# A bidirectional pooling and recurrence block on one core: stores issued by GpSimd, gate and pool products one step later, sums of the last rows made ahead

## The chip, the core and the metric

The kernel runs on one core of a Trainium2 chip. The core has five engines that work side by side, each on its own list of instructions and in the order of that list: TensorE (PE, with PEld for its weight loads), VectorE (DVE), ScalarE (ACT), GpSimd (POOL) and SyncE (SP), which here only issues transfers. An engine that issues a transfer does so in the order of its list as well: when the transfer has to wait for its data, all that stands behind it in that list waits too. The metric is the device time of one execution in microseconds, as the median of a few runs.

## What is computed

One encoder layer over 2048 positions of width 2048, all in float32. Cut to what matters:

```python
h = rms_norm(x, norm_g) * (1 + scale) + shift          # shift, scale, gate = silu(c) @ w_ada + b_ada
z = h @ w_in + b_in                                    # 2048 x 2048 @ 2048 x 4096
u_pool, u_lru, g_pool, g_lru = split(z)                # 1024 columns each
y_pool = pool_mixer(u_pool, w_pool, ...)               # 4 groups of 256: window mean, minus u, @ w_pool
y_lru  = bidir_rg_lru(centred_dwconv(u_lru, ...), ...) # 4 heads of 256: gates = uh @ w_gate, forward + backward scan
y = concat(rms_norm(y_pool) * silu(g_pool), rms_norm(y_lru) * silu(g_lru)) @ w_out + b_out
out = rms_norm(x + gate * y, final_norm_g)             # 2048 x 2048 @ 2048 x 2048
```

## The kernel before

Every product of float32 numbers is made of three: each operand is split into a rounded upper part and the rest (ScalarE copies with rounding, VectorE subtracts, L179 and L180 for the moving operand `m`, L327 and L328 for the stationary operand `s`), and `mm3` (L331) multiplies upper by upper, upper by rest and rest by upper.

**Steps.** One loop runs over `t`, 352 steps of 24 matmuls of 128x512: four output tiles, two slices of the contraction, three products. Steps 0 to 127 make the first half of the input product (four groups of 256 columns of u with their gates), steps 128 to 239 the second half, steps 240 to 351 the output product. The two latter parts save one product in eight by Strassen's method as Winograd wrote it: seven products of half-size blocks (`PRODUCTS`, L134), 56 steps for one pair of column blocks, each product `k` for two halves `q` of the moving side in four slices `p`. `sg` counts the four such sets: 0 and 1 for the input, 2 and 3 for the output. The sums that they need are made by VectorE: of the moving operands in `combine` (L272), of the stationary ones in `unit_split` (L304), of the results in `in_evac` (L478) and `out_evac` (L775). Sums that are used again go to HBM and are loaded back.

**Side work.** The function `at(t, fn, ...)` puts work behind the matmuls of step `t`. A unit of the recurrence (`lru_unit`, L542: one head, direction and block of 512 positions) convolves and splits its input into the only buffer `uch` at step b, multiplies it by the gate weights on TensorE at b+1 and b+2 (`gates`, into the two PSUM buffers `px`), and scans on VectorE at b+4. A unit of the pooling (`pool_unit`, L649) makes window sums at b, multiplies at b+1 (`mix`) and ends at b+2 (`fin`). `rn` (L953) makes the row factors of the group norms, `gate_rows` (L763) spreads the gate over the partitions by four small matmuls. Within its list an engine's order is set at build time by a scheduler with a model of its own, so side work can stand some matmuls before or after where the loop put it.

**Buffers and queues.** `raw` is a ring of eight 512 KB tiles: every load of the loop goes into one, and the results that VectorE makes in place are stored from one, which comes free when the store has landed. SP issues all loads and nearly all stores. Stores of VectorE's results are gathered in a list `late` and issued by SP at the next step, behind that step's loads (L1016 and L1017); ScalarE issues the stores of its own results. Accumulators lie in six PSUM buffers `pm` and two `px`; a product takes four of them, and a buffer is taken again when `in_evac` or `out_evac` has read it. Only in set 3 products 1 and 6 go on adding in the buffers of products 0 and 5 (`CHAINED`, L135), and the second halves `q` use both `px`.

**The end.** After the last product's last step, `out_evac` (L775) adds each of four output tiles to its row block, `part_fin` (L823) multiplies the last quarter of the row by the gate and adds x (which already holds the bias), ScalarE squares and sums it, and `out_row` (L834) scales by the norm and stores.

Of the kernel before, what the change touches and what calls it, by code (L numbers as in the profile page):

```python
# [10 lines left out]
AF = mybir.ActivationFunctionType  # L11
# [34 lines left out]
def layer(ctx: ExitStack, tc: tile.TileContext, xc, xn, c, wada, win, wgate, wpool, wout, vecs, consts, bout, fng, out):  # L46
# [225 lines left out]
    def combine(proj, k, p, q):  # L272
        a, b = wraw.pop(("t", k, q, 0)), wraw.pop(("t", k, q, 1))
        vtt(out=a, in0=a, in1=b, op=ALU.subtract)  # L274
        late.append((moving(proj, f"T{k + 1}", p, q), a))


    rn_t = {}
    late = []

# [18 lines left out]
    def normed(r, tb, k, p):  # L299
        for j in range(2):  # L300
            vtt(out=r[:, j], in0=r[:, j], in1=rn_t[tb, "PL"[k]], op=ALU.mult)  # L301
        late.append((yscr[PAIRS[p + 4 * k]][tb], r))

    def unit_split(u):  # L304
        sg, name, p = unit_args(u)
        rs = yraw.pop(u)
        r = rs[0]
        tb = 2 * (sg - 2)
        if name in ("A11", "A12"):
            if sg > 1:  # L310
                normed(r, tb, int(name[2]) - 1, p)
        elif name == "S2":
            r = rs[1]
            if sg > 1:
# [5 lines left out]
            late.append((sscr[0][p], rs[2]))  # L320
            late.append((sscr[1][p], r))
# [137 lines left out]
    def evac_fix(g, tb):  # L459
        r = R_t.pop(tb)[:, :TB]  # L460
        gr = g_t.pop((g, tb))
        for n in range(4):
            dst = u_t[g][n][:, usl(tb)] if n < 2 else gr[:, n - 2]
            vtt(out=dst, in0=dst, in1=r, op=ALU.mult)
        late.append((gscr[g][tb], gr))

# [11 lines left out]
    def in_evac(sg, k, q, banks):  # L478
# [6 lines left out]
        for n, ps in enumerate(banks):  # L485
            g, i = 4 + 2 * sg + n // 2, n % 2
            bu, bg_ = V("b_in", 4 * g + i), V("b_in", 4 * g + 2 + i)
            lo, hi = u_t[g][i][:, usl(q)], u_t[g][i][:, usl(q + 2)]
            if k == 0:
                act(out=hi, in_=ps, func=AF.Copy)  # L490
            elif k == 1:
                stt(out=lo, in0=ps, scalar=bu, in1=hi, op0=ALU.add, op1=ALU.add)
            elif k == 2:
                vtt(out=hi, in0=ps, in1=hi, op=ALU.add)
            elif k == 3:
                vtt(out=U3[q][:, n], in0=ps, in1=hi, op=ALU.add)
            elif k == 4:
                if i == 0:
                    g_t[g, q] = raw("gr")
                stt(out=g_t[g, q][:, i], in0=U3[q][:, n], scalar=bg_, in1=ps, op0=ALU.add, op1=ALU.subtract)  # L500
                if i == 1:
                    late.append((gscr[g][q], g_t.pop((g, q))))
            elif k == 5:
                stt(out=U3[q][:, n], in0=ps, scalar=bg_, in1=U3[q][:, n], op0=ALU.add, op1=ALU.add)
                vtt(out=hi, in0=ps, in1=hi, op=ALU.add)
                if i == 1:
                    late.append((gscr[g][q + 2], U3[q][:, n - 1:n + 1]))
            else:
                stt(out=hi, in0=ps, scalar=bu, in1=hi, op0=ALU.add, op1=ALU.add)
# [32 lines left out]
    def lru_unit(g, h, d, tb, b, last):  # L542
# [48 lines left out]
        def scan():  # L591
# [21 lines left out]
            if d == 0:  # L613
                late.append((hscr[h][tb], st["h"]))

# [6 lines left out]
        def merge():  # L622
# [4 lines left out]
            for i in range(2):  # L627
# [3 lines left out]
                vtt(out=v, in0=v, in1=hf[:, i], op=ALU.add)  # L631
            late.append((yscr[g][tb], gr))
            if last:
# [4 lines left out]
        at(b, split)  # L638
        at(b + 1, gates, 0)
        at(b + 2, sig, 0)  # L640
        at(b + 2, gates, 1)
        at(b + 3, sig, 1)
        at(b + 3, expo)
        at(b + 4, scan)
        if d == 1:
            at(b + 3, reload)
            at(b + 5, merge)

    def pool_unit(g, q, tb, b, last):  # L649
# [51 lines left out]
        def fin():  # L701
# [7 lines left out]
            for m in range(2):  # L709
# [4 lines left out]
                vtt(out=v, in0=v, in1=y, op=ALU.add)  # L714
            late.append((yscr[g][tb], gr))

        at(b, sums)
        at(b + 1, mix)
        at(b + 2, fin)

# [54 lines left out]
    def out_evac(sg, k, q, banks, tiles):  # L775

        lo, hi = (slice((q + 2 * h) * TB, (q + 2 * h + 1) * TB) for h in range(2))
        for n in tiles:
# [16 lines left out]
            else:  # L795
                vtt(out=b[:, hi], in0=ps, in1=b[:, hi], op=ALU.add)
                if not sg:
                    vtt(out=a[:, hi], in0=ps, in1=a[:, hi], op=ALU.add)

# [23 lines left out]
    def part_fin(sg, n, h, lo, hi, slot):  # L823
# [7 lines left out]
        if hi == 1024:  # L831
            del x_t[sg, n, h]

    def out_row(sg, n, slots, parts):  # L834
        i = row_of(sg, n)
# [8 lines left out]
        for q in range(parts):  # L844
# [4 lines left out]
            else:  # L849
                late.append((out[i * 128:(i + 1) * 128, ds], o))  # L850

# [27 lines left out]
    def gate_fin():  # L879
# [6 lines left out]
    L_AT = {0: [47 + 5 * i for i in range(8)], 2: [87 + 5 * i for i in range(8)],  # L886
            3: [128 + 11 * i // 2 for i in range(8)], 4: [172, 182] + [188 + 5 * i for i in range(6)]}
    P_AT = {1: (75, 80, 85, 90), 5: (164, 180, 184, 186), 6: (221, 236, 242, 248), 7: (224, 239, 245, 251)}
    units = []
# [60 lines left out]

    rn_at = [(228, 0, "P"), (229, 0, "L"), (230, 1, "L"), (231, 2, "L"), (232, 3, "L"), (242, 1, "P"), (248, 2, "P"), (254, 3, "P")]

# [7 lines left out]
    for i in range(4):  # L960
        at(257 + i, gate_rows, i)

# [21 lines left out]
    for t in range(NT):  # L984
# [47 lines left out]
        if key not in banks:  # L1032
            if t == 0:
                banks[key] = [px(), px(), pm(), pm()]
            else:
                banks[key] = [px(), px(), pm(), pm()] if t >= T1 and sg == 3 and q else [pm() for _ in range(4)]
        bk = banks[key]
# [4 lines left out]
        if last:  # L1042
            if t < T1 or sg < 3 or k not in CHAINED.values():
                del banks[key]
# [86 lines left out]
```

## Time and profile before

| | |
|---|---|
| runs, us | 2218.67, 2220.7, 2225.88 (median 2220.7) |
| profiled execution, us | 2217.44 |
| its span, first to last instruction, us | 2215.4 |
| granted TensorE clock, mean | 0.994 |
| TensorE matmul, busy | 2166.2 us, 98% |
| VectorE, busy | 1802.0 us, 81% |
| ScalarE, busy | 1255.3 us, 57% |
| GpSimd, busy | 6.2 us |
| HBM traffic over the span | 276 GB/s |

The profile is one execution. Busy time of TensorE says little by itself, since matmuls are pipelined: one that begins late is seen in the waits and in the distance from start to start. A view of waits lists idle time of an engine by the instruction that ended it; for SP it is the time that its list stood still. "SPq" is an instruction with which SP issues a transfer. A line such as L1017 can stand for many transfers, told apart by the names out<-in.

### The profile page before, as it was taken

The page shows a single profiled execution, that of the slowest core. Times are in us where ns is not written, and L with a number is a line of the kernel's source. Part 1 is how long each engine was busy: PE and PEld are TensorE (multiplying, and loading weights), DVE is VectorE, ACT ScalarE, POOL GpSimd, SP SyncE. Part 2 cuts the span into 40 slices and gives each one's busy share as a digit, 9 for nine tenths or more (in the row PEclk, how much of TensorE's full clock was granted, in tenths as well). Part 3 has the DMA queues.
Part 4 walks back from the last instruction along what each step waited for, and adds up shares of the span by engine and source line. Part 5 has one row for each costly group of instructions (what it writes and reads, how often), then busy time and mean ns, then how long its engine had stood idle before and what let it go on. Part 6 is the DMA issues. An engine that isn't in the chain of part 4 may idle for free. (4 is left out here: it accounts for less than half of the span.)

```text
span 2215.4 us, 25700 instructions
## 1 busy us (share of the span) xinstructions
PE 2166.2 (98%) x9448; PEld 1775.4 (80%) x9448; DVE 1802.0 (81%) x2178; ACT 1255.3 (57%) x1552; POOL 6.2 (0%) x40
## 2 busy tenths in 40 slices
PE   7999999999999999999999999999999999999997
PEld 6888888878788887888888787877877888888886
DVE  7999766578986786867898877979887779967688
ACT  4555578677766676566756666644543333433232
POOL 0000000000000000000000000000000000000000
PEclk9999999999999999999999999999999999999999
DMA  9879945668988897885887787798678756887664
GB/s 389 337 280 334 329 157 200 244 209 294 326 301 311 320 327 278 310 312 200 306 314 257 272 310 275 246 344 297 236 243 308 246 194 235 323 313 289 205 231 171
DMA packets 161342, 613.22 MB, mean 277 GB/s; under 512 B 17856, under 2 KB 19136, under 8 KB 153280
## 3 DMA queue, kind: packets, MB, share of 16 engines
q1 hardware_dynamic: 154880, 588.51, 74.2%
q10 hardware_dynamic: 6336, 23.07, 2.7%
q8 instruction: 74, 1.21, 0.2%
q14 instruction: 52, 0.43, 0.1%
HBM read 467.85 MB, written 143.65 MB: 276 GB/s over the span
## 5 line engine op out<-in xcount | busy, mean ns | idle before, releaser
L334 PE MATMUL pm<-m,s 128*128 128x512 f32 x8004 | 1857.8, 391 | 7.9 <-DVE sum L788 7.9
L334 PEld LDWEIGHTS pm<-m,s 128*128 128x128 f32 x8004 | 1506.3, 188 | 330.7 <-DVE sum L788 8.7
L179 ACT ACTIVATE m<-xr 128x1024 fp32r<-128x1024 f32 x350 | 369.3, 1055 | 499.0 <-PE pm L334 323.1
L180 DVE TENSOR_TENSOR m<-xr,m 128x1024 fp32r<-128x1024 f32 x350 | 426.9, 1221 | 131.9 <-ACT m L179 125.2
L334 PE MATMUL px<-uch,gw 128*128 128x512 f32 x768 | 191.4, 394 | 9.4 <-ACT uch L563 5.2
L334 PEld LDWEIGHTS px<-uch,gw 128*128 128x128 f32 x768 | 143.6, 189 | 45.6 <-DVE uch L564 8.4
L327 ACT ACTIVATE s<-yr 128x1024 fp32r<-128x1024 f32 x104 | 109.5, 1054 | 92.3 <-DMA yr<-in_win_dram 27.1
L328 DVE TENSOR_TENSOR s<-yr,s 128x1024 fp32r<-128x1024 f32 x104 | 126.9, 1221 | 22.3 <-ACT s L327 22.3
L334 PE MATMUL px<-m,s 128*128 128x512 f32 x420 | 105.0, 394 | 13.0 <-ACT m L383 12.4
L402 DVE CUSTOM_DVE_ANT_0 ada<-ada,cact 128x2048 f32<-128x2048 f32 x47 | 107.4, 2288 | 10.4 <-DMA ada<-in_wada_dram 10.4
L274 DVE TENSOR_TENSOR tr<-tr 128x1024 f32<-128x1024 f32 x64 | 78.3, 1224 | 45.3 <-DMA tr<-xs 16.9
L334 PEld LDWEIGHTS px<-m,s 128*128 128x128 f32 x420 | 79.1, 190 | 30.6 <-ACT m L383 12.4
L579 DVE TENSOR_TENSOR ig<-ig,u 128x512 f32<-128x512 f32 x64 | 44.2, 691 | 36.8 <-ACT ig L577 36.8
L598 DVE SCALAR_TENSOR_TENSOR th<-rg,th 128x512 f32<-128x512 f32 x64 | 42.7, 686 | 36.6 <-ACT th L593 36.6
L195 ACT ACTIVATE xr<-xr,shv 128x512 f32<-128x512 f32 x64 | 44.0, 717 | 24.6 <-DVE xr L194 23.5
L334 PE MATMUL px<-uch,pw 128*128 128x512 f32 x192 | 50.0, 398 | 5.1 <-ACT uch L687 3.7
L563 ACT ACTIVATE uch<-u 128x512 fp32r<-128x512 f32 x64 | 38.4, 624 | 26.3 <-DVE u L558 26.0
L577 ACT ACTIVATE ig<-px,vec 128x512 f32<-128x512 f32 x64 | 43.8, 684 | 15.5 <-PE px L334 15.1
L577 ACT ACTIVATE rg<-px,vec 128x512 f32<-128x512 f32 x64 | 43.9, 686 | 12.7 <-PE px L334 12.3
L194 DVE SCALAR_TENSOR_TENSOR xr<-xr,sc,rl 128x512 f32<-128x512 f32 x64 | 45.5, 750 | 6.9 <-DMA xr<-in_xc_dram 6.9
L821 DVE TENSOR_TENSOR x<-x,gb 128x1024 f32<-128x1024 f32 x32 | 39.0, 1223 | 14.4 <-DMA x<-in_xn_dram 14.4
L558 DVE SCALAR_TENSOR_TENSOR cv<-u,vec,cv 128x512 f32<-128x512 f32 x64 | 44.9, 748 | 6.8 <-ACT cv L556 6.7
(183 smaller groups left out, 1715.7 us busy)
## 6 DMA issues: line engine op xcount, KB each, us to landing
xr<-xs SPq DMA_DIRECT2D x112, 512.0 KB, 5.6
ada<-in_wada_dram SPq DMA_DIRECT2D x47, 1024.0 KB, 7.7
yr<-in_win_dram SPq DMA_DIRECT2D x72, 512.0 KB, 5.4
yr<-ys SPq DMA_DIRECT2D x72, 512.0 KB, 4.7
xr<-h SPq DMA_DIRECT2D x64, 512.0 KB, 5.6
xr<-t SPq DMA_DIRECT2D x64, 512.0 KB, 4.8
xr<-in_xc_dram SPq DMA_DIRECT2D x63, 512.0 KB, 6.6
tr<-xs SPq DMA_DIRECT2D x48, 512.0 KB, 5.8
```

Of the source, the lines that this page charges most:

```text
L179: act(out=m[:, 0], in_=r, func=AF.Copy)
L180: vtt(out=m[:, 1], in0=r, in1=mf[:, 0], op=ALU.subtract)
L194: stt(out=r[:, j], in0=r[:, j], scalar=sc[:, k:k + 1], in1=rr, op0=ALU.mult, op1=ALU.mult)
L195: act(out=r[:, j], in_=r[:, j], func=AF.Identity, bias=shv[:, k:k + 1])
L274: vtt(out=a, in0=a, in1=b, op=ALU.subtract)
L327: act(out=s[:, 0], in_=r, func=AF.Copy)
L328: vtt(out=s[:, 1], in0=r, in1=s.bitcast(F32)[:, 0], op=ALU.subtract)
L334: nc.tensor.matmul(out=ps, lhsT=a[:, x, j, asl], rhs=b[:, y, j], start=first and i == 0, stop=last and i == 2, skip_group_check=more)
L402: nc.vector.tensor_tensor_reduce(out=t, in0=t, in1=cact["t"], op0=ALU.mult, op1=ALU.add, scale=1.0, scalar=0.0, accum_out=mod[:, i:i + 1])
L558: stt(out=a if k < 3 else U[i][:, us], in0=src, scalar=cw, in1=a, op0=ALU.mult, op1=ALU.add)
L577: act(out=v, in_=st.pop(("ps", w, i)), func=AF.Sigmoid, bias=V("b_gate", (d * 4 + h) * 4 + 2 * w + i))
L579: vtt(out=st["i", i], in0=st["i", i], in1=U[i][:, us], op=ALU.mult)
```

## The change

1. The list `late` is gone. GpSimd issues the stores that went through it (`keep`), as soon as the result is there; in the built program it has 202 of them.
2. Gate products, their sigmoids and the scan come one step later in their unit, the reload and merge of the backward direction too; so do `mix` and `fin` of the pooling. Three tables of start steps are adjusted (`L_AT`, `P_AT`, `rn_at`), and `gate_rows` runs at 257, 257, 258, 259.
3. In set 2, product 6 goes on adding in the buffers of product 5, so eight additions of 128x512 fall away; from product 2 on, second halves use `px` there too.
4. For the last four row blocks, gate times sum plus x is made at steps 332 to 335 (`last_pre`); behind the last matmuls only the last product times gate is added (`last_fin`), and each row is finished behind the next row's addition.

```diff
+    keep = nc.gpsimd.dma_start
     def combine(proj, k, p, q):
-        late.append((moving(proj, f"T{k + 1}", p, q), a))
+        keep(out=moving(proj, f"T{k + 1}", p, q), in_=a)
...
     # in the same way: normed, unit_split, evac_fix, in_evac, scan, merge, fin, out_row
...
-        for dst, src in late:
-            store(out=dst, in_=src)
-        late.clear()
...
-        at(b + 1, gates, 0)
-        at(b + 2, sig, 0)
-        at(b + 2, gates, 1)
-        at(b + 3, sig, 1)
-        at(b + 3, expo)
-        at(b + 4, scan)
+        at(b + 2, gates, 0)
+        at(b + 3, sig, 0)
+        at(b + 3, gates, 1)
+        at(b + 4, sig, 1)
+        at(b + 4, expo)
+        at(b + 5, scan)
         if d == 1:
-            at(b + 3, reload)
-            at(b + 5, merge)
+            at(b + 4, reload)
+            at(b + 6, merge)
...
         at(b, sums)
-        at(b + 1, mix)
-        at(b + 2, fin)
+        at(b + 2, mix)
+        at(b + 3, fin)
...
-                if not sg:
-                    vtt(out=a[:, hi], in0=ps, in1=a[:, hi], op=ALU.add)
...
+    def last_pre(n):
+        ds = slice(3 * TB, 4 * TB)
+        o = C_t[1, n][:, ds]
+        vtt(out=o, in0=o, in1=fin["gate"][:, ds], op=ALU.mult)
+        vtt(out=o, in0=o, in1=x_t[1, n, 1][:, TB:], op=ALU.add)
+
+    def last_fin(n, ps):
+        ds = slice(3 * TB, 4 * TB)
+        o = C_t[1, n][:, ds]
+        v = x_t.pop((1, n, 1))[:, TB:]
+        vtt(out=v, in0=ps, in1=fin["gate"][:, ds], op=ALU.mult)
+        vtt(out=o, in0=o, in1=v, op=ALU.add)
+        act(out=v, in_=o, func=AF.Square, accum_out=ssq[:, row_of(1, n), 2:3])
...
-            more = sg == 3 and k in CHAINED
+            more = k in CHAINED and (sg == 3 or sg == 2 and k == 6)
...
-                    out_evac(sg - 2, k, q, bk, (i,))
-                    part_fin(sg - 2, i, 1, TB, 2 * TB, 2)
-                    out_row(sg - 2, i, 3, 4 if i == 3 else 2)
+                    last_fin(i, bk[i])
+                    if i:
+                        out_row(1, i - 1, 3, 2)
+                out_row(1, 3, 3, 4)
```

Three places in the engines' lists, before and after. First TensorE, around step 130, at the first gate products (`px<-uch,gw`) of the head whose units begin at step 128; 24 matmuls `pm<-m,s` are one step. Before:

```order
L334 MATMUL px<-uch,gw 128x512 x12
L334 MATMUL pm<-m,s 128x512 x120
L334 MATMUL px<-uch,gw 128x512 x2
L334 MATMUL pm<-m,s 128x512 x5
L334 MATMUL px<-uch,gw 128x512 x10
L334 MATMUL pm<-m,s 128x512 x19
L334 MATMUL px<-uch,gw 128x512 x12
```

The same place after the change:

```order
L334 MATMUL px<-uch,gw 128x512 x12
L334 MATMUL pm<-m,s 128x512 x120
L334 MATMUL px<-uch,gw 128x512 x12
L334 MATMUL pm<-m,s 128x512 x24
L334 MATMUL px<-uch,gw 128x512 x12
L334 MATMUL pm<-m,s 128x512 x96
```

Each block of products stands one step later (step 131 where it was 130, counted from the start), and is in one piece. SP's list at the same steps, before (`h` and `ys` are results that are stored, `gl` and `tr` the tiles they come from, the other rows are loads):

```order
L269 DMA tr<-xs_7_288 128x1024
L1017 DMA h_3_0_239<-tr 128x1024
L269 DMA tr<-xs_3_284 128x1024
L1017 DMA ys_0_161<-gl 128x1024
L167 DMA xr<-xs_3_260 128x1024
L167 DMA xr<-xs_0_265 128x1024
L296 DMA yr<-in_win_dram 128x1024
L167 DMA xr<-xs_1_266 128x1024
L1017 DMA h_3_1_240<-tr 128x1024
```

After:

```order
L270 DMA tr<-xs_7_288 128x1024
L270 DMA tr<-xs_3_284 128x1024
L618 DMA hl<-hs_0_141 128x1024
L620 DMA gl<-gs_0_113 128x1024
L168 DMA xr<-xs_3_260 128x1024
L168 DMA xr<-xs_0_265 128x1024
L296 DMA yr<-in_win_dram 128x1024
L168 DMA xr<-xs_1_266 128x1024
```

The stores have left SP's list; what is left there waits for free tiles and for stored data that is loaded back, no longer for a result that is still to be made. Second, VectorE where product 1 of set 2 is read out of PSUM for its second half (L788, steps 255 to 259). Before:

```order
L180 TENSOR_TENSOR m<-xr,m 128x1024
L788 TENSOR_TENSOR sum<-pm,sum 128x512
L319 TENSOR_TENSOR yc<-yr 128x1024
L419 RECIPROCAL sqP<-sqP 128x512
L328 TENSOR_TENSOR s<-yc,s 128x1024
L788 TENSOR_TENSOR sum<-pm,sum 128x512
L788 TENSOR_TENSOR o<-pm,o 128x512 x2
```

After:

```order
L181 TENSOR_TENSOR m<-xr,m 128x1024
L328 TENSOR_TENSOR s<-yc,s 128x1024
L788 TENSOR_TENSOR sum<-pm,sum 128x512 x2
L788 TENSOR_TENSOR o<-pm,o 128x512 x2
L181 TENSOR_TENSOR m<-xr,m 128x1024
L319 TENSOR_TENSOR yc<-yr 128x1024
L419 RECIPROCAL sqP<-sqP 128x512
```

The four read-outs stand together, ahead of the reciprocal. Third, the end of VectorE's list. Before:

```order
L846 SCALAR_TENSOR_TENSOR sum<-sum,rst,fg 128x1024 x2
L840 TENSOR_TENSOR rst<-ssq 128x1
L790 TENSOR_TENSOR o<-pm,o 128x512
L842 RECIPROCAL rst<-rst 128x1
L828 TENSOR_TENSOR o<-o,gate 128x512
L846 SCALAR_TENSOR_TENSOR o<-o,rst,fg 128x1024 x2
L829 TENSOR_TENSOR o<-o,x 128x512
L840 TENSOR_TENSOR rst<-ssq 128x1
L842 RECIPROCAL rst<-rst 128x1
L846 SCALAR_TENSOR_TENSOR o<-o,rst,fg 128x512 x4
```

After:

```order
L859 SCALAR_TENSOR_TENSOR sum<-sum,rst,fg 128x1024 x2
L853 TENSOR_TENSOR rst<-ssq 128x1
L843 TENSOR_TENSOR x<-pm,gate 128x512
L855 RECIPROCAL rst<-rst 128x1
L844 TENSOR_TENSOR o<-o,x 128x512
L859 SCALAR_TENSOR_TENSOR o<-o,rst,fg 128x1024 x2
L853 TENSOR_TENSOR rst<-ssq 128x1
L855 RECIPROCAL rst<-rst 128x1
L859 SCALAR_TENSOR_TENSOR o<-o,rst,fg 128x512 x4
```

For the last row one operation fewer stands behind the last matmul, and its last addition stands ahead of the scaling of the row before it.

## Rows read from the trace of the kernel before

**Rows 1.** Page: busy us; then 100 us of PE, PEld, DVE, ACT, POOL, clock.
```profile
PE 2166.2 (98%) x9448; PEld 1775.4 (80%) x9448; DVE 1802.0 (81%) x2178; ACT 1255.3 (57%) x1552; POOL 6.2 (0%) x40
...
1500.00:1600.00 100.00, 100.00 (x434) 81.22 (x433) 92.49 (x105) 49.81 (x61) 0.00 (x0) 1.00 0.75 263
```

**Rows 2.** TensorE's waits: who for whom, us in total, times, longest.
```profile
PE pm L334 <- DVE sum L788: 7.9, 2, 4.1
PE px L334 <- ACT uch L563: 5.2, 4, 2.8
PE px L334 <- DVE uch L564: 4.2, 7, 1.3
PE px L334 <- ACT uch L687: 3.7, 2, 2.2
```

**Rows 3.** The chain that ended last: start, us, line and count of merged matmuls.
```profile
1707.21 211.51 PE pm L334 x933
```

**Rows 4.** TensorE at two gate products: start, us, [idle before, and who ended it].
```profile
835.02 0.72 PE L334 MATMUL px<-uch,gw 128*128 128x512 f32 x2 [2.81 <-ACT uch L563]
835.58 2.28 PE L334 MATMUL pm<-m,s 128*128 128x512 f32 x5
837.66 2.66 PE L334 MATMUL px<-uch,gw 128*128 128x512 f32 x8
...
1133.22 0.73 PE L334 MATMUL px<-uch,gw 128*128 128x512 f32 x2 [1.40 <-ACT uch L563]
```

**Rows 5.** SP's list, the transfers issued ahead of the wait at 832 us.
```profile
822.24 0.32 SPq L1017 DMA_DIRECT2D ys<-gl  x1
...
825.68 0.96 SPq L296 DMA_DIRECT2D yr<-in_win_dram  x1
```

**Rows 6.** ScalarE, what held it ahead of the same wait.
```profile
833.39 1.06 ACT L327 ACTIVATE s<-yr 128x1024 fp32r<-128x1024 f32 x1 [3.92 <-DMA yr<-in_win_dram]
```

**Rows 7.** Waits of SP's own list: us in total, times, longest.
```profile
SPq L296 <- DVE m L180: 165.5, 61, 7.1
...
SPq L1017 <- DVE carry L612: 75.8, 7, 27.7
```

**Rows 8.** VectorE, 1600 to 1682 us, at the read-outs of product 1 of set 2.
```profile
1625.80 0.69 DVE L301 TENSOR_TENSOR yr<-yr,sqP 128x512 f32<-128x512 f32 x1 [3.91 <-DMA yr<-ys]
...
1672.03 3.35 DVE L419 RECIPROCAL sqP<-sqP 128x512 f32<-128x512 f32 x1
```

**Rows 9.** TensorE at the same read-outs, two stretches.
```profile
1644.78 4.51 PE L334 MATMUL pm<-m,s 128*128 128x512 f32 x12 [4.12 <-DVE sum L788]
...
1677.10 11.50 PE L334 MATMUL pm<-m,s 128*128 128x512 f32 x39 [3.76 <-DVE sum L788]
```

**Rows 10.** The last matmuls.
```profile
2200.17 1.52 PE L334 MATMUL pm<-ml,s 128*128 128x512 f32 x6
```

**Rows 11.** VectorE behind them.
```profile
2203.15 0.68 DVE L790 TENSOR_TENSOR o<-pm,o 128x512 f32<-128x512 f32 x1
...
2204.47 2.47 DVE L846 SCALAR_TENSOR_TENSOR o<-o,rst,fg 128x1024 f32<-128x1024 f32 x2
2206.87 0.68 DVE L829 TENSOR_TENSOR o<-o,x 128x512 f32<-128x512 f32 x1
2208.34 0.16 DVE L840 TENSOR_TENSOR rst<-ssq 128x1 f32<-128x1 f32 x1 [0.79 <-ACT x L830]
...
2209.06 2.74 DVE L846 SCALAR_TENSOR_TENSOR o<-o,rst,fg 128x512 f32<-128x512 f32 x4
```

**Rows 12.** GpSimd, its longest instruction.
```profile
200.44 1.81 POOL L539 MEMSET sqL<- 128x2048 f32 x1 [1.35 <-DVE mod L402]
```

**Rows 13.** VectorE beside it.
```profile
201.43 1.23 DVE L255 TENSOR_TENSOR s<-wr,s 128x1024 fp32r<-128x1024 f32 x1
```

**Rows 14.** The stores of line 1017: issue time ns min/median/max of one kind; landing of all.
```profile
L1017 SPq DMA_DIRECT2D h<-tr x32: 319/422/518, 403.0 to 881.1; - x32
...
DMA to landing us min/median/max: 2.6/5.5/9.1
```

More of the change, by code (lines that the diff above doesn't have):

```diff
@@ L274, in combine @@
         vtt(out=a, in0=a, in1=b, op=ALU.subtract)
-        late.append((moving(proj, f"T{k + 1}", p, q), a))
+        keep(out=moving(proj, f"T{k + 1}", p, q), in_=a)
     rn_t = {}
-    late = []
     def unit_args(u):
@@ L301, in normed @@
             vtt(out=r[:, j], in0=r[:, j], in1=rn_t[tb, "PL"[k]], op=ALU.mult)
-        late.append((yscr[PAIRS[p + 4 * k]][tb], r))
+        keep(out=yscr[PAIRS[p + 4 * k]][tb], in_=r)
     def unit_split(u):
@@ L319, in unit_split @@
             vtt(out=r, in0=rs[1], in1=rs[2], op=ALU.subtract)
-            late.append((sscr[0][p], rs[2]))
-            late.append((sscr[1][p], r))
+            keep(out=sscr[0][p], in_=rs[2])
+            keep(out=sscr[1][p], in_=r)
         elif name == "S4":
@@ L464, in evac_fix @@
             vtt(out=dst, in0=dst, in1=r, op=ALU.mult)
-        late.append((gscr[g][tb], gr))
+        keep(out=gscr[g][tb], in_=gr)
     def evac(g, tb, banks):
@@ L501, in in_evac @@
                 if i == 1:
-                    late.append((gscr[g][q], g_t.pop((g, q))))
+                    keep(out=gscr[g][q], in_=g_t.pop((g, q)))
             elif k == 5:
@@ L506, in in_evac @@
                 if i == 1:
-                    late.append((gscr[g][q + 2], U3[q][:, n - 1:n + 1]))
+                    keep(out=gscr[g][q + 2], in_=U3[q][:, n - 1:n + 1])
             else:
@@ L613, in scan @@
             if d == 0:
-                late.append((hscr[h][tb], st["h"]))
+                keep(out=hscr[h][tb], in_=st["h"])
         def reload():
@@ L631, in merge @@
                 vtt(out=v, in0=v, in1=hf[:, i], op=ALU.add)
-            late.append((yscr[g][tb], gr))
+            keep(out=yscr[g][tb], in_=gr)
             if last:
@@ L714, in fin @@
                 vtt(out=v, in0=v, in1=y, op=ALU.add)
-            late.append((yscr[g][tb], gr))
+            keep(out=yscr[g][tb], in_=gr)
         at(b, sums)
-        at(b + 1, mix)
-        at(b + 2, fin)
+        at(b + 2, mix)
+        at(b + 3, fin)
     def softplus():
@@ L849, in out_row @@
             else:
-                late.append((out[i * 128:(i + 1) * 128, ds], o))
+                keep(out=out[i * 128:(i + 1) * 128, ds], in_=o)
     AHEAD = 4
@@ L886, in layer @@
     L_AT = {0: [47 + 5 * i for i in range(8)], 2: [87 + 5 * i for i in range(8)],
-            3: [128 + 11 * i // 2 for i in range(8)], 4: [172, 182] + [188 + 5 * i for i in range(6)]}
-    P_AT = {1: (75, 80, 85, 90), 5: (164, 180, 184, 186), 6: (221, 236, 242, 248), 7: (224, 239, 245, 251)}
+            3: [128 + 11 * i // 2 for i in range(8)], 4: [172] + [187 + 5 * i for i in range(7)]}
+    P_AT = {1: (75, 80, 85, 90), 5: (164, 180, 183, 185), 6: (221, 236, 242, 248), 7: (224, 239, 245, 251)}
     units = []
@@ L924, in layer @@
                 at(b + 50 + n, out_row, sg, n + 4, 2, 1)
+                at(b + 36 + n, last_pre, n)
                 at(b + 53 + n // 2, part_fin, sg, n, 1, 0, TB, 1)
@@ L949, in rn @@
         nc.vector.reciprocal(out=v, in_=v)
-    rn_at = [(228, 0, "P"), (229, 0, "L"), (230, 1, "L"), (231, 2, "L"), (232, 3, "L"), (242, 1, "P"), (248, 2, "P"), (254, 3, "P")]
+    rn_at = [(229, 0, "P"), (230, 0, "L"), (231, 1, "L"), (232, 2, "L"), (233, 3, "L"), (243, 1, "P"), (249, 2, "P"), (255, 3, "P")]
     def rn(tb, kind):
@@ L960, in layer @@
     for i in range(4):
-        at(257 + i, gate_rows, i)
+        at(257 + i * 3 // 4, gate_rows, i)
     unit_at = {T1 - 6 + 2 * u: u for u in range(112)}
@@ L1035, in layer @@
             else:
-                banks[key] = [px(), px(), pm(), pm()] if t >= T1 and sg == 3 and q else [pm() for _ in range(4)]
+                banks[key] = [px(), px(), pm(), pm()] if q and t >= T1 and (sg == 3 or sg == 2 and k > 1) else [pm() for _ in range(4)]
         bk = banks[key]
@@ L1042, in layer @@
         if last:
-            if t < T1 or sg < 3 or k not in CHAINED.values():
+            if t < T1 or sg < 2 or k not in CHAINED.values() or sg == 2 and k == 0:
                 del banks[key]
```

## The prediction

> **What bounds the kernel now.** I read the page first. TensorE is busy 98% of the span, VectorE 81%, ScalarE 57% [rows 1]. The chain that ended last shows the pace: 933 matmuls in one stretch in 211.51 us [rows 3], 0.2267 us each, or 5.44 us for a step of 24. All 9448 matmuls [rows 1] at that pace are 2141.9 us. Only what TensorE loses beyond this, and the start and the tail, can be won. So the next view is TensorE's waits [rows 2]. Two families matter: gate and pool products (`px`) wait for `uch`, 5.2 + 4.2 + 3.7 = 13.1 us in 13 waits, and products of set 2 wait twice for a PSUM buffer that VectorE has not read out (L788), 7.9 us. No row of that view names `m`: the main operands come in time.
>
> A wait costs more than its length. At 1133 us two matmuls behind a wait took 0.73 us instead of 0.45 [rows 4]: 0.28 us for a restart. Behind the longest wait, 2.81 us at 832, 15 matmuls took 5.30 us (835.02 to 840.32) instead of 3.40: 1.9 us more [rows 4]. The five right behind the first two are the slowest, 2.28 us or 0.46 each. Behind the two L788 waits, 12 matmuls took 4.51 us instead of 2.72 and 39 took 11.50 instead of 8.84 [rows 9]: 1.8 and 2.66 us more.
>
> Then the cause. Ahead of 832 us ScalarE stood 3.92 us until a load of `in_win` landed [rows 6]. SP had issued this load at 825.68, and right ahead of it in SP's list stands a store, issued at 822.24 [rows 5]. SP's waits show what such stores do: seven of them, behind the scan's result, hold SP's list for 75.8 us in all, one for 27.7 [rows 7]. But SP also waits 165.5 us for free tiles (L296 behind `m`) [rows 7], which no issuer changes. At the read-outs it is the same picture: VectorE idles 3.91 us at 1625 for a reload `yr<-ys`, and a 3.35 us reciprocal at 1672 stands between the first and the second read-out [rows 8].
>
> **The change part by part.**
>
> *Products a step later.* The lists show each block of `px` products one step, 5.44 us, further back, while the convolution and split that feed them stay. The longest wait is 2.81 us [rows 4], so a step covers each wait where the block has moved. What is removed: 13.1 us of waits, 12 restarts at 0.28 us = 3.4, and 1.9 at 832, together 18.4. The product behind the wait of 1.40 us at 1133 [rows 4] stands in the same step in both lists, so 1.40 + 0.28 = 1.7 may stay: **16.7**. Bounds: 18.4, and 0 if the producers slide along (rival C). The scan, reload and merge come a step later too; what they feed is the row factors `rn`, needed by the output product. The tables that place `rn` move with them, and the lists show its reciprocals where they were. Costed at nothing; if that cover is gone, one step, 5.4 us, at step 240.
>
> *Stores on GpSimd.* SP loses 202 issues at about 0.42 us [rows 14], and the waits in front of them. GpSimd works 6.2 us in the whole span [rows 1], so its list is free to stand still. What is queued behind a waiting store is now only other stores. These hold tiles of the ring until they land, in the median 5.5 us after issue [rows 14]. The order among stores is nearly as before and they no longer wait for the next step's loads, so tiles come free no later. By itself this wins nothing on TensorE; it is what makes reloads and `in_win` loads early enough for the two other terms. The issue on GpSimd is not shown in this trace. Bounds: as on SP, 0.42 us of an idle engine, hence nothing; or as GpSimd's longest instruction, 1.81 us [rows 12], still off the path (202 x 1.81 = 366 us of 2215), unless VectorE is held meanwhile (rival D). Beside that 1.81 us instruction, a VectorE operation took 1.23 us [rows 13], so it was not held for the other's length. I take nothing.
>
> *Set 2.* The four read-outs of product 1 come together in VectorE's list, and the reciprocal behind them; the loads ahead are no longer behind stores. The eight additions that fall away are 8 x 0.68 = 5.4 us of VectorE, and as many come in with `last_pre`, beside matmuls whose operands are not late; costed at nothing both ways, 5.4 us if VectorE had no room. To be won are 7.9 us [rows 2] + 1.8 + 2.66 [rows 9] = 12.4. The second stall (3.76 + 2.66 = 6.4) loses the reciprocal of 3.35 us, nearly its wait; the first (4.12 + 1.8 = 5.9) goes only if the reloads come earlier by about 4 us. VectorE stays near full here. I take two thirds, **8**; bounds 0 and 12.4.
>
> *The tail.* The last matmul ends at 2200.17 + 1.52 = 2201.69 [rows 10]. Today the last row's addition starts at 2203.15, the scaling of row 2 (2.47 us) comes before L829, and the four last pieces start at 2209.06, 0.72 us after `rst` at 2208.34 [rows 11]. After: two operations of 0.68 (as L790 and L829) from 2201.7 to 2203.05, row 2's scaling until 2205.5, and beside it ScalarE's square, which today makes VectorE idle 0.79 us [rows 11]. Then 0.72 until the pieces: 2206.2. Gain **2.9**; bounds 2.1 (the 0.79 stays) and 2.9.
>
> **Sum.** 16.7 + 8 + 2.9 = 27.6 us. Against the profiled execution: 2217.4 - 27.6 = 2189.8. That execution lies 3.3 us below the median of the runs; against the median, 2220.7 - 27.6 = **2193**.
>
> **The rivals.**
>
> *B: the stores leave SP, but loads come no earlier*, since SP then waits for free tiles in their place: the 165.5 us for L296 [rows 7] speaks for it, the store at 822.24 right ahead of the late load [rows 5] against it. The L788 term falls to nothing, the products still have their step: 16.7 + 2.9 = 19.6, or 2201. The row says that SP's list lost 75.8 us to seven stores which were not ready. The Trainium skill, "DMA: Bandwidth & Descriptors", section "Issuing engines are not separate DMA queues", has it that issuing from several engines saves only the sequencer's time to initiate, usually small; by it the gain here would be 202 issues on SP and B would hold. The trace of before disagrees in part, since the loss is the standing behind results, which that sentence leaves out.
>
> *C: the producers slide along.* ScalarE and VectorE take the free step for other work, and `px` still waits for `uch`. For it: VectorE is 92.5% busy at 1500 to 1600 [rows 1]. Against: the seven waits for VectorE's `uch` are 1.3 us at the longest [rows 2], a quarter of the step that is given. Gain 8 + 2.9 = 10.9: 2210.
>
> *D: slower, VectorE held by GpSimd's issues.* If each store took GpSimd 1.81 us [rows 12] and VectorE stood still for it, the 9 stores of 100 us (202 over 22 such stretches) would cost 16.3 us, where VectorE has 7.5 idle at 1500 to 1600 [rows 1]: 8.8 us short, in each of the five stretches that are over 90% full, 44 us. With 10.9 of gains left: 2254. It decides from 7.5 / 9 = 0.8 us of VectorE per store. Against it stands the undisturbed 1.23 us [rows 13], but that was one instruction, and no store. The Trainium skill, "SBUF — State Buffer", section "SBUF: two separate sides", says that the two share a port pair as an exclusive lock, and that some VectorE operations keep GpSimd from writing descriptors; the operations that it names there, copies in a two-port mode, hardly occur here, and no run yet shows it.
>
> *E: the change doesn't do what it says.* GpSimd's list is in order too: behind the scan's late result (27.7 us) [rows 7] other stores pile up, ring tiles stay taken, and SP's loads stand as long as today. The shift's gain is spent on later operands: 2221. Against: on SP the same store held the same successors and the loads as well.
>
> **How the numbers follow.** Forecast A 0.58, B 0.16, C 0.10, D 0.10, E 0.06. A's own range is 2187 (18.4 + 12.4 + 2.9 = 33.7 gained) to 2201 (half of the products' term not gained: 8.4 + 8 + 2.9 = 19.3). The range reaches from 2183, since runs of before spread by 2 below and 5 above their median, to C's 2210; it leaves out D and E and a little of A. About 0.3%, 6.7 us, is what a measurement of this kernel can tell from no change: A, B and C are faster by more (0.84), E is no change (0.06), D slower (0.10).
>
> **What would show it.** Products: in the waits, `px` behind `uch` at most 3 us in all, instead of 13.1; C if they stay above 8. Stores: SP's rows for stores gone, and no `yr` load behind one; B if L296 and the reloads wait longer by what the stores waited. Set 2: `pm` behind L788 below 4.5 us. Tail: the four last pieces start 4.5 us behind the last matmul instead of 7.4. D: the same VectorE operations (1.23 us, 0.68 us) longer in the mean, beside GpSimd's issues. The forecast is wrong if `pm` begins to wait for `m`, since then a load or a sum that was in time has become late.

## The result and the profile after

The changed kernel takes 2313.5 us (median of 4 runs, 2311.2 to 2315.9); the kernel before takes 2219.7 beside it. The ratio is 1.042, with an interval of 1.040 to 1.044: 94 us slower, where 28 us faster was forecast.

The page of the profile after, with the columns of [rows 1]; the second line is the queue that GpSimd's stores use:

```profile
PE 2203.0 (95%) x9448; PEld 1790.9 (77%) x9448; DVE 1800.7 (78%) x2174; ACT 1241.6 (54%) x1548; POOL 117.1 (5%) x248
...
q0 software_dynamic: 29952, 115.36, 12.6%
```

VectorE works as long as before (1800.7 against 1802.0 us), so its operations got no longer; it stands idle about 100 us longer. GpSimd, at 117 us, is far from full. The trace has 208 stores on it (248 instructions against 40), not 202. TensorE's waits, with the columns of [rows 2]:

```profile
PE pm L334 <- DVE gr L500: 14.7, 4, 10.3
...
PE px L334 <- DVE uch L564: 11.2, 10, 2.0
PE px L417 <- DVE sqP L714: 7.7, 2, 5.5
PE px L334 <- ACT uch L563: 7.2, 7, 2.1
PE px L334 <- ACT pw L665: 5.7, 1, 5.7
PE px L334 <- DVE m L181: 5.4, 2, 5.0
...
PE pm L334 <- DVE sum L788: 1.5, 2, 0.9
```

The waits at the read-outs of set 2 have shrunk from 7.9 to 1.5 us, but the products still wait for `uch`, and there are new waits of every kind: for read-outs (`gr`, L500), for sums of squares, even for the split of the moving operand `m`, which was not late before. Most of what is late is made by VectorE, so VectorE itself is held up. What holds it is seen in the groups of its instructions by line. First the kernel before (busy, mean ns | idle time just before them, and what ended it), the sums of two loaded tiles in `combine` and the scaling of reloaded ones in `normed`:

```profile
L274 DVE TENSOR_TENSOR tr<-tr 128x1024 f32<-128x1024 f32 x64 | 78.3, 1224 | 45.3 <-DMA tr<-xs 16.9 <-DMA tr<-in_wout_dram 8.2 <-DMA tr<-t 7.4
...
L301 DVE TENSOR_TENSOR yr<-yr,rn 128x512 f32<-128x512 f32 x32 | 21.1, 686 | 7.7 <-DMA yr<-ys 7.6
```

The same groups after:

```profile
L275 DVE TENSOR_TENSOR tr<-tr 128x1024 f32<-128x1024 f32 x64 | 78.1, 1220 | 74.8 <-DMA tr<-xs 45.1 <-DMA tr<-in_wout_dram 15.9 <-DMA tr<-h 7.4
...
L301 DVE TENSOR_TENSOR yr<-yr,rn 128x512 f32<-128x512 f32 x32 | 20.8, 685 | 29.4 <-DMA yr<-ys 29.4
```

The durations are the same, the idle time in front is 30 and 22 us more, and loads end it. Summed over all of VectorE's waits in the trace, loads end 140 us of idle time before and 243 after; ScalarE ends 243 and 242.

One place shows how this reaches TensorE. VectorE in the kernel before, in set 3:

```profile
1958.97 1.22 DVE L180 TENSOR_TENSOR m<-xr,m 128x1024 fp32r<-128x1024 f32 x1
1963.86 1.23 DVE L180 TENSOR_TENSOR m<-xr,m 128x1024 fp32r<-128x1024 f32 x1 [3.67 <-ACT m L179]
1966.10 2.56 DVE L301 TENSOR_TENSOR yr<-yr,rn 128x512 f32<-128x512 f32 x4 [1.02 <-DMA yr<-ys]
1970.79 1.22 DVE L318 TENSOR_TENSOR yr<-yr 128x1024 f32<-128x1024 f32 x1 [2.13 <-DMA yr<-ys]
```

And after, at the same four scalings (the 57th to 60th of the 64 operations of L301), 90 us later by the clock:

```profile
2049.42 1.22 DVE L181 TENSOR_TENSOR m<-xr,m 128x1024 fp32r<-128x1024 f32 x1
2056.03 1.29 DVE L301 TENSOR_TENSOR yr<-yr,rn 128x512 f32<-128x512 f32 x2 [5.39 <-DMA yr<-ys]
2059.74 1.29 DVE L301 TENSOR_TENSOR yr<-yr,rn 128x512 f32<-128x512 f32 x2 [2.42 <-DMA yr<-ys]
2060.95 1.22 DVE L181 TENSOR_TENSOR m<-xr,m 128x1024 fp32r<-128x1024 f32 x1
```

TensorE there:

```profile
2056.86 0.39 PE L334 MATMUL px<-m,s 128*128 128x512 f32 x1
2062.22 5.06 PE L334 MATMUL px<-m,s 128*128 128x512 f32 x11 [4.98 <-DVE m L181]
```

Before, two `m` stand ahead of the four scalings, so the wait for the reload falls where TensorE has its operand already. After, the scalings stand ahead of the second `m`; VectorE waits 5.39 + 2.42 us for reloads, and the `m` behind them comes 5 us too late. SP's list looks as was hoped for, none of the 208 stores in it. But its loads now wait elsewhere (columns of [rows 7]):

```profile
SPq L168 <- DVE m L181: 168.6, 62, 12.2
SPq L296 <- DVE m L181: 155.7, 57, 8.7
...
SPq L168 <- DMA t<-tr: 72.7, 13, 7.9
```

The last row is a load that waits until a store has landed and given its tile of the ring back; before, such waits of L167 for `t` came to 17.4 us. Over the whole trace, SP's waits ahead of its own stores fall from 404 to 66 us, and the waits of its loads for landed transfers rise from 352 to 764. These by themselves are no measure of a loss: in the second run below, which is 59 us faster than the first, they are 69 and 727 us.

### The profile page after: what moved, and what is told of

Same layout as the page of the kernel before. It is cut to its first block, busy times and chain, and to the rows that moved or that the text cites. A ratio compares the mean times of both kernels' runs of the same rounds, so it can differ in the third digit from the quotient of the medians.

```text
span 2314.0 us, 26000 instructions
## 1 busy us (share of the span) xinstructions
PE 2203.0 (95%) x9448; PEld 1790.9 (77%) x9448; DVE 1800.7 (78%) x2174; ACT 1241.6 (54%) x1548; POOL 117.1 (5%) x248
## 3 DMA queue, kind: packets, MB, share of 16 engines
q0 software_dynamic: 29952, 115.36, 12.6%
## 4 chain that ended last, share of the span: by engine, by line
PE 21%; DMA 11%; issue 9%; DVE 8%; ACT 3%; POOL 0%; DVEq 0%; SPq 0%; POOLq 0%; ACTq 0%
PE pm L334 15%; PE px L334 6%; DMA yr<-ys 2%; DVE m L181 2%; DMA gl<-gs 1%; DMA yr<-ss 1%; DMA yr<-in_win_dram 1%; DMA t<-tr 1%; DMA ys<-gl 1%; DMA tr<-in_wout_dram 1%; DVE s L328 1%; DMA ss<-yr 0%; DMA pwr<-in_wpool_dram 0%; DMA gs<-gr 0%; ACT m L180 0%
## 5 line engine op out<-in xcount | busy, mean ns | idle before, releaser
L334 PE MATMUL pm<-m,s 128*128 128x512 f32 x7764 | 1815.9, 393 | 31.2 <-DVE gr L500 14.7
L334 PEld LDWEIGHTS pm<-m,s 128*128 128x128 f32 x7764 | 1467.2, 189 | 354.2 <-DVE gr L500 16.3
L181 DVE TENSOR_TENSOR m<-xr,m 128x1024 fp32r<-128x1024 f32 x350 | 425.7, 1217 | 125.4 <-ACT m L180 123.3
L334 PE MATMUL px<-uch,gw 128*128 128x512 f32 x768 | 200.8, 408 | 28.1 <-DVE uch L564 11.2
L334 PE MATMUL px<-m,s 128*128 128x512 f32 x660 | 166.2, 397 | 18.6 <-ACT m L383 12.6
L334 PEld LDWEIGHTS px<-m,s 128*128 128x128 f32 x660 | 125.5, 191 | 47.6 <-ACT m L383 12.6
L275 DVE TENSOR_TENSOR tr<-tr 128x1024 f32<-128x1024 f32 x64 | 78.1, 1220 | 74.8 <-DMA tr<-xs 45.1
L402 DVE CUSTOM_DVE_ANT_0 ada<-ada,cact 128x2048 f32<-128x2048 f32 x47 | 107.3, 2285 | 13.2 <-DMA ada<-in_wada_dram 13.1
L819 DVE TENSOR_TENSOR x<-x,gb 128x1024 f32<-128x1024 f32 x32 | 38.8, 1220 | 25.5 <-DMA x<-in_xn_dram 25.2
L334 PEld LDWEIGHTS px<-uch,pw 128*128 128x128 f32 x192 | 38.1, 202 | 25.0 <-DVE uch L688 6.1
L629 ACT ACTIVATE hl<-hl 128x512 f32<-128x512 f32 x32 | 20.1, 630 | 66.5 <-DVE gl L628 66.2
L828 ACT ACTIVATE x<-o 128x1024 f32<-128x1024 f32 (+1 forms) x24 | 24.6, 1026 | 54.4 <-DVE o L827 44.0
```

What stands on the lines that cost most here:

```text
L181: vtt(out=m[:, 1], in0=r, in1=mf[:, 0], op=ALU.subtract)
L334: nc.tensor.matmul(out=ps, lhsT=a[:, x, j, asl], rhs=b[:, y, j], start=first and i == 0, stop=last and i == 2, skip_group_check=more)
L402: nc.vector.tensor_tensor_reduce(out=t, in0=t, in1=cact["t"], op0=ALU.mult, op1=ALU.add, scale=1.0, scalar=0.0, accum_out=mod[:, i:i + 1])
L819: vtt(out=r, in0=r, in1=fin["gb"][:, h * 1024:(h + 1) * 1024], op=ALU.add)
```

## The experiments

The first question was which part of the change does it: the stores or the shift of steps. The stores in turn do two things. They change who issues at run time, and they change what the scheduler makes of the program. In the built lists of the kernel with the stores alone moved, `combine`, `normed`, the sums of `unit_split` and the addition of the bias to x stand 0.42, 0.61, 0.38 and 0.31 of a step earlier on the mean than before, counted by how many `m` splits stand ahead of them in VectorE's list. Three theories: O, the order of the lists holds VectorE behind loads that have not landed; T, issue by GpSimd makes stores and thereby tiles late; S, the step shift. The kernel before was measured again beside each run, at medians from 2219.3 to 2222.6 us, so differences of 3 us between runs mean nothing.

**The stores alone**, from the kernel before:

```diff
-        late.append((moving(proj, f"T{k + 1}", p, q), a))
+        keep(out=moving(proj, f"T{k + 1}", p, q), in_=a)
...
-        for dst, src in late:
-            store(out=dst, in_=src)
-        late.clear()
```

> The kernel before with one edit: VectorE's stores are issued by GpSimd at once; no step is shifted, no sum moved. The built lists differ from before's: VectorE's sums and scalings of loaded tiles (combine, normed, unit_split, x plus bias) stand 0.3 to 0.6 of a step earlier on the mean. Theory O (the changed lists hold VectorE up behind loads that have not landed): most of the 94 us of loss shows here, 2270 to 2310 us, and VectorE's idle time ended by loads grows by some 80 us. Theory T (GpSimd's issue and the landing of its stores are slower): the same time. Theory S (the step shift does it): 2195 to 2225.

Measured: 2291.8 us, ratio 1.033 (1.031 to 1.036), +72 us. S falls. Its groups show the loss at the same lines:

```profile
L275 DVE TENSOR_TENSOR tr<-tr 128x1024 f32<-128x1024 f32 x64 | 78.1, 1220 | 74.9 <-DMA tr<-in_wout_dram 32.7 <-DMA tr<-xs 24.8 <-DMA tr<-h 8.5
...
L301 DVE TENSOR_TENSOR yr<-yr,rn 128x512 f32<-128x512 f32 x32 | 21.2, 686 | 26.8 <-DMA yr<-ys 26.8
```

**The same with the lists pinned.** Every engine's instructions get an edge to the one that should stand ahead of them, of issue order alone, so that no wait is added. The table `ORDER` holds, engine by engine, the order that the kernel before has, for SP that of its loads; `mine` are the engine's instructions as the program is written, `d` how far each is moved.

```diff
+    for e, text in ORDER.items():
...
+        row = [mine[k + v] for k, v in enumerate(d)]
+        for a, b in zip(row, row[1:]):
+            tc.add_manual_dep(b, a.name, mybir.DependencyInfo(mybir.DependencyClass.NoSync, mybir.DependencyReason.DATA), reason="pin")
...
+    pin(tc)
```

> As the run with the stores alone on GpSimd, but the lists of TensorE, VectorE, ScalarE and SP's loads are pinned to the order of the kernel before by edges that carry no wait. Theory O: the loss goes, 2200 to 2225 us. Theory T: it stays within 15 us of the unpinned run, since each store is still issued by GpSimd. Theory S: no difference from the unpinned run, both at 2195 to 2225.

Measured: 2233.2 us, ratio 1.006 (1.004 to 1.008). Of the 72 us, 59 are gone with the stores still on GpSimd; 13 are left, more than O alone allows, and the time lies far below what T allows. The groups are back near those of before:

```profile
L338 DVE TENSOR_TENSOR tr<-tr 128x1024 f32<-128x1024 f32 x64 | 78.0, 1219 | 39.5 <-DMA tr<-xs 23.2 <-DMA tr<-h 5.5 <-DMA tr<-in_wout_dram 4.8
...
L364 DVE TENSOR_TENSOR yr<-yr,rn 128x512 f32<-128x512 f32 x32 | 21.2, 685 | 12.4 <-DMA yr<-ys 12.4
```

With equal lists, loads can be compared one by one: by the number of `m` matmuls that TensorE had begun when SP issued a load, the 854 loads are issued 0.01 of a step earlier than before, on the mean. With the lists held, taking the stores out of SP's list brought the loads forward by nothing.

**The shift alone**, from the kernel before, with its three tables of start steps:

```diff
-        at(b + 1, gates, 0)
+        at(b + 2, gates, 0)
...
-        at(b + 1, mix)
+        at(b + 2, mix)
```

> The kernel before with one edit: gate and pool products, and what follows them, a step later, with the three tables of start steps; stores stay on SP. Theories O and T: 2195 to 2225 us, waits of px for uch less than the 13.1 us of before by up to 10. Theory S: 2270 or more.

Measured: 2211.6 us, ratio 0.996 (0.995 to 0.998): 8 us faster. **All but the stores**, the changed kernel with the list `late` put back:

```diff
-        keep(out=moving(proj, f"T{k + 1}", p, q), in_=a)
+        late.append((moving(proj, f"T{k + 1}", p, q), a))
...
+        for dst, src in late:
+            store(out=dst, in_=src)
+        late.clear()
```

> The changed kernel with the stores given back to SP, behind the next step's loads; shift, added accumulation in set 2 and the tail stay. Theories O and T: 2190 to 2215 us, faster than before by the tail's 3 us and part of the 12 us at the read-outs of set 2. Theory S: 2270 or more.

Measured: 2208.8 us, ratio 0.995 (0.994 to 0.997): 11 us faster than before, the lowest median here. TensorE's waits in it:

```profile
PE pm L334 <- DVE gr L500: 7.9, 3, 4.6
PE px L334 <- DVE uch L564: 3.8, 4, 2.0
PE px L334 <- ACT uch L563: 3.5, 2, 2.1
PE px L770 <- DVE dg L767: 2.4, 1, 2.4
```

The products' waits for `uch` have gone from 13.1 to 7.3 us, the two at L788 are gone, and in their place stand waits for other read-outs. At the longest, TensorE and VectorE read:

```profile
1466.31 8.87 PE L334 MATMUL pm<-m,s 128*128 128x512 f32 x26 [4.62 <-DVE gr L500]
...
1457.76 2.46 DVE L608 TENSOR_TENSOR_SCAN th<-rg,carry,ig 128x512 f32<-128x512 f32 x2
...
1462.45 1.41 DVE L628 SCALAR_TENSOR_TENSOR gl<-hl,vec,gl 128x512 f32<-128x512 f32 x2
...
1465.51 1.40 DVE L500 SCALAR_TENSOR_TENSOR gr<-sum,vec,pm 128x512 f32<-128x512 f32 x2
```

The scan and merge, moved with the products, now stand ahead of the read-out for which TensorE waits 4.62 us.

**The changed kernel with the lists of the last one.** Stores are on GpSimd; `ORDER` holds the lists of the kernel with all but the stores.

```diff
+    pin(tc)
```

> The changed kernel with GpSimd's stores, but the lists of TensorE, VectorE, ScalarE and SP's loads pinned to the order that the run with all but the stores had (2208.8 us). Theory O (lists): the 104 us between that run and the changed kernel shrink to what pinning left in the stores-alone case, 13 us: 2215 to 2230. Theory T (GpSimd's issue, made worse by the shift): 2260 or more.

Measured: 2238.7 us, ratio 1.009 (1.007 to 1.011). So of the 105 us between the changed kernel and the one with all but the stores, the lists make 75, and issue by GpSimd 30. The 30 is more than twice the 13 that were expected, and the time lies in neither range.

**The reverse:** the kernel before, all stores on SP; `ORDER` holds the lists of TensorE, VectorE and ScalarE from the run with the stores alone:

```diff
+    pin(tc)
```

> The reverse: the kernel before with all stores on SP, and the lists of TensorE, VectorE and ScalarE pinned to the order of the run with the stores alone on GpSimd (2291.8 us). Theory O: the lists alone bring the loss, 2265 to 2295 us. If the lists do harm only together with GpSimd's stores: 2215 to 2235.

Measured: 2292.4 us, ratio 1.033 (1.031 to 1.035). This is the run that settles it: no store is on GpSimd, and the time is that of the run with the stores alone, to 0.6 us. Loads end 242 us of VectorE's idle time here, as they end 245 with the stores alone and 140 before. With these lists, issue by GpSimd adds nothing (2291.8 against 2292.4), with the lists of before held it costs 13: the two do not simply add.

```profile
L332 DVE TENSOR_TENSOR tr<-tr 128x1024 f32<-128x1024 f32 x64 | 78.2, 1221 | 81.0 <-DMA tr<-in_wout_dram 35.7 <-DMA tr<-t 13.7 <-DMA tr<-xs 13.4
...
L359 DVE TENSOR_TENSOR yr<-yr,rn 128x512 f32<-128x512 f32 x32 | 21.2, 686 | 23.1 <-DMA yr<-ys 22.9
```

**Whose list?** The stores alone on GpSimd, with some lists pinned to the kernel before and the others left to the scheduler. `ORDER` with VectorE's alone:

```diff
+    pin(tc)
```

> Stores alone on GpSimd, with VectorE's list alone pinned to that of the kernel before; TensorE's, ScalarE's and SP's lists are left to the scheduler. If VectorE's list is what held the kernel up: within 8 us of the fully pinned run, 2225 to 2241. If ScalarE's or SP's order has a share: 2245 to 2285.

Measured: 2266.4 us, ratio 1.023 (1.020 to 1.026). `ORDER` with all but VectorE's (TensorE, ScalarE, SP's loads):

```diff
+    pin(tc)
```

> Stores alone on GpSimd; TensorE's, ScalarE's and SP's lists pinned to those of the kernel before, VectorE's left to the scheduler, which puts its sums of loaded tiles 0.2 to 0.5 of a step earlier. Unpinned 2291.8, fully pinned 2233.2, VectorE's list alone pinned 2266.4. If VectorE's list holds its own 25 us and the other lists 33: 2250 to 2270. If VectorE's list brings all of it and the others follow: 2280 to 2295. If harm comes only where ScalarE's list has moved too: 2228 to 2245.

Measured: 2276.6 us, ratio 1.025 (1.023 to 1.027), between the first two ranges. `ORDER` with VectorE's and ScalarE's:

```diff
+    pin(tc)
```

> Stores alone on GpSimd; VectorE's and ScalarE's lists pinned to those of the kernel before, TensorE's and SP's left to the scheduler. If the 33 us that stayed with VectorE's list alone pinned stand in ScalarE's list (splits of loaded tiles ahead of others): 2228 to 2242. If they come from the 8 loads that moved in SP's list or from TensorE's order: 2255 to 2275.

Measured: 2240.1 us, ratio 1.009 (1.006 to 1.011). Against the fully pinned 2233.2, VectorE's order by itself costs 43 us; the other lists by themselves cost 33, of which ScalarE's, where splits of loaded tiles stand in one list with the copies of `m` and `uch`, holds 26. The parts sum to 77, more than the 59 that they cost together, as would follow if both often wait for the same load; that was not traced. The idle time in front of ScalarE's splits of `yr` falls with the second pin. VectorE's list alone pinned, and then both:

```profile
L365 ACT ACTIVATE s<-yr 128x1024 fp32r<-128x1024 f32 x104 | 109.4, 1053 | 128.5 <-DMA yr<-in_win_dram 37.3 <-DVE yr L363 24.4 <-DVE yr L357 20.3
```

```profile
L377 ACT ACTIVATE s<-yr 128x1024 fp32r<-128x1024 f32 x104 | 109.3, 1052 | 105.9 <-DMA yr<-in_win_dram 35.3 <-DVE yr L375 22.8 <-DVE yr L369 21.4
```

**Does SP's standing behind late results cost anything?** The kernel with all but the stores, pinned to its own lists, with the 16 stores of the scan's result given to GpSimd. In the kernel before SP stood 75.8 us behind seven of them [rows 7]; in the kernel with all but the stores it is (columns of [rows 7]):

```profile
SPq L1031 <- DVE hf L604: 48.4, 8, 14.4
SPq L1031 <- DVE carry L612: 47.1, 7, 17.6
```

The edit takes both rows away:

```diff
-                late.append((hscr[h][tb], st["h"]))
+                nc.gpsimd.dma_start(out=hscr[h][tb], in_=st["h"])
```

> The run with all but the stores (2208.8 us), lists pinned to its own, with 16 stores alone, those of the forward scan's result (hs), given to GpSimd. They made SP stand 75.8 us in 7 waits in the kernel before. If SP's standing behind unfinished results delays loads that TensorE needs: 2198 to 2206. If a load has to wait for a free tile of the ring anyway: 2206 to 2213.

Measured: 2210.2 us, ratio 0.996 (0.994 to 0.998), as the 2208.8 without the edit. Of the 95 us of standing no gain shows; the intervals leave room for some 5 us. The run also shows that pinning by itself costs no more than that.

**Which stores carry the 30 us?** The same with the 64 stores of `combine`:

```diff
-        late.append((moving(proj, f"T{k + 1}", p, q), a))
+        nc.gpsimd.dma_start(out=moving(proj, f"T{k + 1}", p, q), in_=a)
```

> The run with all but the stores (2208.8 us), its lists pinned, with 64 stores alone, those of combine (h and t), given to GpSimd. All 208 there cost 30 us in the pinned run (2238.7). If each store on GpSimd costs alike: 30 x 64 / 208 = 9, or 2218. If it is these stores, which hold tiles of the ring and landed 0.7 us later: 2225 to 2240. If they cost nothing: 2205 to 2213.

Measured: 2222.3 us, ratio 1.000 (0.999 to 1.001): 13 us of the 30 by the medians, 5 to 14 by the ratios. The share in number (9) lies within that, all 30 does not; the median itself lies in none of the three ranges. What makes issue by GpSimd cost 13 us (lists of the kernel before) to 30 us (shifted lists) is open. Loads end more of VectorE's idle time in these runs (155 us here and 169 with all stores, against 135). Late stores, as theory T has it, are not seen to be the reason: counted in the traces from the result on, the 64 stores of `combine` have landed after 7.3 us on the mean here and 7.4 with all stores on GpSimd, against 8.0 with none there. Kernels with an added delay ahead of each store, or with a ring of another size, were not tried.

## Why the prediction was wrong, point by point

**Stores on GpSimd: the step that failed.** The prediction took this part at nothing, and bounded it by the engine time of an issue. It cost 105 us: as pinning splits it, 75 through the lists and 30 through the issue itself. Both causes that the prediction weighed for a loss are small or absent. GpSimd's issue takes 0.53 us, inside the bounds, and 0.67 at the longest, and VectorE's operations are no longer than before (1220 against 1224 ns for `combine`), which rules out rival D's mechanism though its sign came true. The lock of which the Trainium skill tells ("SBUF — State Buffer", section "SBUF: two separate sides") lengthened no VectorE operation here. What was left out is that the edit changes every list. The prediction read the new lists at the products, the read-outs and the tail, and took the rest as unmoved; it did not ask where VectorE's consumers of loads now stand against `m`. They stand 0.3 to 0.6 of a step earlier, as if loads came sooner by as much; by the count used above, loads are issued 0.14 of a step earlier in the run with the stores alone, and 0.01 with the lists held. The lists alone bring 73 us to the kernel before. That the scheduler's model puts the consumers there because stores no longer hold SP is argued from the lists of the one-edit kernel, not from its model. The sign that the prediction named for being wrong, `pm` waiting for `m`, came true (2.0 us for L181, and 4.0 for ScalarE's part of `m`).

**Loads come no earlier.** Here rival B was right, and the argument against it wrong. The store at 822 us does not stand right ahead of the late load [rows 5]; two other loads stand between them in SP's list before:

```profile
822.65 2.78 SPq L167 DMA_DIRECT2D xr<-xs  x2
```

The second of them waited 2.0 us for a tile that an `m` split gave back at 825.06, so in this trace the late load, issued at 825.68, could not have come much earlier without the store. The loads' mean shift of 0.01 step, and the 16 scan stores whose move gained nothing, say that the 75.8 us [rows 7] were no loss to TensorE. The Trainium skill, "DMA: Bandwidth & Descriptors", section "Issuing engines are not separate DMA queues", says that issuing from another engine saves only the sequencer's time; the prediction put the trace against it, and the runs bear it out: moving the issues gained nothing.

**Products a step later: 16.7 forecast.** Three things were misread. The lists of the kernel with the shift alone put the products 1.5 steps later on the mean, but the splits of `uch` 0.8 later, presumably since they wait for the only buffer `uch`, which is now held longer; the slack won is 0.8 of a step, not one, and the waits fell by 5.8 us (13.1 to 7.3), not by 11 or more. And the scan and merge moved 2 steps on the mean, into the way of read-outs: 7.9 us of new waits at L500. "Costed at nothing" was wrong there; the cover was VectorE's idle time, which the view of a whole span does not place. Third, the restart of 0.28 us compares the length of a row, which holds all of its last matmul (0.39 us for one alone, above), with the distance from start to start. By the starts in [rows 4] the two matmuls at 835.02 take 0.56 us instead of 0.45, so a restart is 0.11 us and the 12 of them 1.3, not 3.4. The shift alone is worth 8 us.

**Set 2: 8 forecast, bounds 0 and 12.4.** With all but the stores, no wait at L788 is left, and 2.4 us came back as a wait for `dg`, which stands near it. But with the shift alone no wait at L788 is left either (and 3.9 us for `dg`), so they went with its lists and not with the edit of set 2. From there to all but the stores it is 3 us, as much as the tail; nothing clear of noise is left for set 2. Without the stores the parts were forecast at 27.6 us together; they gave 11.

**The tail: 2.9 forecast.** TensorE and VectorE at the end after:

```profile
2301.58 1.52 PE L334 MATMUL pm<-ml,s 128*128 128x512 f32 x6
...
2303.14 0.69 DVE L843 TENSOR_TENSOR x<-pm,gate 128x512 f32<-128x512 f32 x1 [0.34 <-PE pm L334]
...
2304.48 2.47 DVE L859 SCALAR_TENSOR_TENSOR o<-o,rst,fg 128x1024 f32<-128x1024 f32 x2
...
2307.38 0.16 DVE L855 RECIPROCAL rst<-rst 128x1 f32<-128x1 f32 x1 [0.36 <-ACT rst L854]
2307.58 2.74 DVE L859 SCALAR_TENSOR_TENSOR o<-o,rst,fg 128x512 f32<-128x512 f32 x4
```

The last matmul ends at 2301.58 + 1.52 = 2303.10, and the four pieces start 4.48 us behind it, where it was 7.37 [rows 10, 11]: 2.9 us, as worked out.

**Rival C** was half right: producers do slide along, by half of the shift. **Rival E** named stores piling up on GpSimd behind the scan; they do not, since in the trace after each of the 64 stores of `combine` and the 32 of `normed` is issued 0.41 us behind its result. No rival had the lists in it, so 2254 for the slower side was a right sign from a wrong cause, with 0.10 for it; where a build step decides the order, that chance should have been larger, since the lists were there to be compared.

**What a long wait costs** was not foreseen for a kernel with many of them. From 1540 to 1560 us after, and from 1550 to 1555 alone, with the columns of [rows 1]:

```profile
1540.00:1560.00 20.00, 13.46 (x40) 9.29 (x39) 13.97 (x19) 8.35 (x11) 1.06 (x2) 0.74 0.96 328
...
1550.00:1555.00 5.00, 4.14 (x8) 2.11 (x9) 4.51 (x6) 2.69 (x4) 0.00 (x0) 0.50 0.91 309
```

TensorE waits 5.7 us there for `pw` (L665), until 1549.77. The mean granted clock of the stretch is 0.74; from 1550 to 1555 it is 0.50, the lower of the two levels, 1.2 GHz. In all, from its first matmul on, TensorE loses 149 us against its pace of 0.2267 us a matmul, 87 of them in the waits of [rows 2]'s view; before, it lost 47, with 23 in waits. The mean granted clock fell from 0.994 to 0.979.

**A row passed over.** "No row of that view names `m`" is not so; the view of before begins with one:

```profile
PE px L334 <- ACT m L383: 12.4, 1, 12.4
```

It is the wait for the first operand, at the start of the kernel. It is 12.6 us after, so nothing in the forecast hangs on it.

## What to carry to other kernels

When a scheduler orders the lists, an edit that only changes who issues a transfer can be an edit of every list: compare, for each engine that TensorE depends on, where the consumers of loads stand against the operations that TensorE waits for, before anything else is costed. An issuing engine that stands still was no loss by itself here; ask which resource the transfers behind it need, since if that is a free buffer, unblocking the issuer may move nothing. To tell an order from a mechanism, pin the lists and change only the mechanism, and then do the reverse.

## What the runs showed of the hardware

Most kinds of store took longer from issue to landing when GpSimd issued them. In the first pinned run the stores of `combine` landed in the median 7.4 us after their issue (`h`), against 6.0 on SP, and those of the scan 6.0 against 3.0; and GpSimd begins an issue 0.41 us after the result that it waited for, where SP begins within 0.07. But SP's stores stood behind its loads first: from the result to the landing, the stores of `combine` took 7.5 us on the mean in that run and 8.1 in the kernel before, those of `normed` 6.3 and 9.4, those of the scan 5.9 and 4.0. The issue itself after the change:

```profile
L276 POOL DMA_DIRECT2D h<-tr x32 | 17.1, 533 | 253.8 <-DVE tr L275 253.8
```

It takes 0.53 us against 0.42 [rows 14]. The Trainium skill, "DMA: Bandwidth & Descriptors", section "Latency and other measured facts", gives a first byte of about 1 us on this path and about 0.6 on SP's. No run here times a first byte; the medians from issue to landing differ by -0.7 to 3.0 us by the kind of store, more than the 0.4 us between those two figures.
